# Two layers of attention on one core: modulation weights in one-k-tile pieces, other landing times in the planner, other warm-up counts, and the instruction order that follows

## The chip, the cores and the metric

The kernel runs on one core of a Trainium2 chip. The metric is the device time of one execution in microseconds. The core has a matrix engine (PE, with its weight loads listed as PEld), a vector engine (DVE), a scalar engine (ACT), a general engine (POOL) and a queue engine (SP), which issues nearly all transfers from DRAM here. Each engine works through its own list of instructions in order; semaphores tie the lists together.

## The reference

Input x has 256 rows of 1024 numbers, c is one row of 1024. Two layers follow each other, an NSA layer and a MoBA layer. Each is normalised, modulated by a vector computed from c, mixed, and added to x with a gate:

```python
cond = jax.nn.silu(c)
for i in range(DEPTH):
    shift, scale, gate = jnp.split(cond @ ada_w[i] + ada_b[i], 3, axis=-1)
    h = rms_norm(x, norm_g[i]) * (1 + scale[:, None, :]) + shift[:, None, :]
    y = mixer(h, ...)
    x = x + gate[:, None, :] * y
```

The first mixer projects h by w_in (queries, six key and value blocks, gate logits, an output gate z), compresses keys and values into 15 blocks, selects blocks, attends in three ways, multiplies by silu(z) and projects by w_out. The second has one causal attention over the 256 rows with the same z and w_out. All matrices are float32. The products of h with a weight are made of three products of rounded parts: with hi the rounded number and lo the rest, hi times hi, hi times lo and lo times hi.

## The kernel before, in words

Contraction runs over 1024 = 8 k tiles of 128. A tile `HT` holds h transposed, hi and lo, for all 8 k tiles. Weight pieces are loaded into buffers of 128 x 1024 floats (`early`, 12 of them, in the first stage; `raw`, 5, later), ACT casts a piece to `hi` (four buffers), DVE subtracts to get `lo` (four buffers), and PE multiplies.

**The first stage** (from line 1216 on, `START`) builds h of layer 0 in pieces of two k tiles, because the modulation weights arrive in pieces too. `load_stage("s", k0)` loads eight 256 KB pieces, one for each k tile of c, holding shift and scale for the h tiles k0 and k0+1. For k0 = 0 and 6 `ada_start` turns them into a row with products on PE (tile `ps<-early,condz`), copies it to SBUF (ACT, tile `row`) and transposes it (`ada_columns`); for k0 = 2 and 4 `ada_summed` adds the eight pieces up on DVE (eight operations on `row`, 128 x 512 each) and sums over partitions on PE with a column of ones. Either way DVE then writes the columns `AB`, and ACT (hi) and DVE (through `rot`, lo) write two k tiles of `HT`. `load_stage("k", k0)` loads the NSA weights of two k tiles in four pieces: ci 0 (key and value before compression, goes to `acc`), ci 1 and 2 (the other keys and values) and ci 3 (256 columns of queries, half the size).

**Later modulation** (the gate of layer 0 and shift and scale of layer 1) comes from `ada_rows`, called three times. It adds up eight k tiles of a 1 x 1024 row in one PSUM tile, four products for each k tile, each on 32 columns of the array. A piece is 512 KB.

**Warm-up.** `SPINS` products whose result nobody reads are put on PE twice: on x (`ps<-X,identF`) before the first modulation products, and on the first `row` (`ps<-row,identF`).

**The order.** Nothing is issued as it is written. `Plan` records every operation and `issue` lays them out with a list scheduler: per engine it takes, among the operations that can start, the one with the lowest number in `TURNS` (one number for each operation, some 2400). When an operation can start comes from a cost model inside the kernel: for a load, the time on the wire (`RATE`, with factors for short rows such as 1.06) plus `LANDED`. These figures, `TURNS` and the buffer counts fix the order of each engine when the kernel is built; on the chip nothing is chosen any more. All operations carry line 543 (545 after the change), where the recorded calls are issued, so rows are told apart by their tiles.

Of the kernel before, what the change touches and what calls it, by code (L numbers as in the profile page):

```python
# [18 lines left out]
P = 128  # L19
S = 256  # L20
D = 1024
# [18 lines left out]
WRITTEN = 2500.0  # L40
TURNS = [
# [528 lines left out]
def kernel(  # L570
# [265 lines left out]
    def ada_rows(l, cs):  # L836

        acc = tile_of("ps", 256)
        for kk in range(0, 8, 2):
# [4 lines left out]
            if kk < 6:  # L844
                yield
# [860 lines left out]
```

## Time and profile before

| | us |
|---|---|
| median of 3 runs | 311.52 |
| lowest, highest | 309.72, 1549.1 |
| the profiled execution | 312.38 |
| its span, first to last instruction | 310.7 |
| PE busy in it | 290.5 |
| DVE busy in it | 254.9 |
| ACT busy in it | 195.9 |

The profiled execution took 312.38 us, its span 310.7 us; the 1.7 us between lie around the first and last instruction. Times inside the profile are counted from the first instruction. In the timeline a row merges instructions of the same kind that follow each other: its start, how long the row lasts, engine, operation, output tile and input tiles, shape, count, and in brackets how long the engine sat idle before it and what ended that. A product of float32 operands leaves two records. "x16" of the 32-column products is 8 products.

### The profile page before, as it was taken

How to read it: one execution, taken by the hardware profiler on the slowest of the kernel's cores; microseconds unless marked ns; L12 is line 12 of the kernel's file. 1: busy time of each engine (PE TensorE's matmuls, PEld its weight loads, DVE VectorE, ACT ScalarE, POOL GpSimd, SP SyncE). 2: the span in 40 equal slices, each digit the busy share in tenths (PEclk: the TensorE clock that was granted, in tenths of full speed). 3: DMA queues.
4: the chain of work that ended last, by engine and by line, in shares of the span. 5: the costliest groups of instructions: out<-in, count | busy, mean ns of one | idle time of the engine just before them, and what ended most of it. 6: DMA issues, size and time to landing. Idle time of an engine off the chain costs nothing.

```text
span 310.7 us, 6923 instructions
## 1 busy us (share of the span) xinstructions
PE 290.5 (93%) x2597; PEld 238.7 (77%) x2597; DVE 254.9 (82%) x529; ACT 195.9 (63%) x467; POOL 27.7 (9%) x99
## 2 busy tenths in 40 slices
PE   4679999999999998999998999989998998999995
PEld 4567877787766777788778887767886997997884
DVE  2279984679994798899986978896799999999965
ACT  4364351484457747999658935768593898399530
POOL 7000007890000000000000000010000000000000
PEclk9999989999999999999999999999999999999999
DMA  7999999256979978394999799433789673467603
GB/s 261 293 361 354 346 365 364 82 166 198 354 214 333 324 210 256 126 340 167 361 270 204 176 228 302 184 92 113 208 262 312 203 214 126 138 142 197 138 0 135
DMA packets 49728, 70.83 MB, mean 228 GB/s; under 512 B 4908, under 2 KB 29087, under 8 KB 49696
## 3 DMA queue, kind: packets, MB, share of 16 engines
q1 hardware_dynamic: 49528, 70.34, 72.8%
q8 instruction: 20, 0.33, 0.5%
q14 instruction: 12, 0.10, 0.1%
q10 hardware_dynamic: 168, 0.06, 0.1%
HBM read 67.76 MB, written 2.62 MB: 227 GB/s over the span
## 4 chain that ended last, share of the span: by engine, by line
PE 56%; DVE 19%; DMA 13%; ACT 5%; issue 4%; SPq 1%; ACTq 0%; DVEq 0%
PE ps L543 34%; PE acc L543 22%; DVE lo L543 7%; DVE p L543 5%; DMA raw<-in_ada_w_dram 4%; DMA raw<-in_moba_w_in_dram 3%; DMA early<-in_nsa_w_in_dram 3%; DMA raw<-in_nsa_w_in_dram 2%; ACT hi L543 2%; DMA y<-in_norm_g_dram 2%; SPq L543 1%; DVE tiny L543 1%; DVE row L543 1%; ACT p L543 1%; DVE rs L543 1%
## 5 line engine op out<-in xcount | busy, mean ns | idle before, releaser
L543 ACT CAST hi<-raw 128x1024 fp32r<-128x1024 f32 (+1 forms) x50 | 51.3, 1030 | 19.9 <-PE acc L543 8.5
L543 DVE TENSOR_TENSOR lo<-raw,hi 128x1024 fp32r<-128x1024 f32 (+1 forms) x50 | 58.8, 1183 | 4.4 <-ACT hi L543 4.3
L543 PE MATMUL acc<-HT,hi 128*128 128x256 f32 x256 | 50.8, 289 | 1.8 <-DVE zT L543 1.4
L543 PE MATMUL acc<-hi,HT 128*128 128x512 f32 (+1 forms) x160 | 50.3, 383 | 0.8 <-ACT HT L543 0.8
L543 ACT ACTIVATE p<-ps,tiny 128x128 f32<-128x128 f32 (+1 forms) x96 | 39.9, 447 | 6.7 <-DVE tiny L543 6.6
L543 PEld LDWEIGHTS acc<-HT,hi 128*128 128x128 f32 x256 | 40.5, 189 | 4.3 <-DVE zT L543 1.8
L543 PE MATMUL acc<-HT,lo 128*128 128x256 f32 x128 | 36.2, 289 | 0.0
L543 PE MATMUL ps<-hi,HT 128*128 128x512 f32 (+1 forms) x112 | 35.2, 381 | 0.5 <-ACT HT L543 0.5
L543 PEld LDWEIGHTS acc<-hi,HT 128*128 128x128 f32 x160 | 28.9, 188 | 7.5 <-ACT HT L543 1.0
L543 PE MATMUL acc<-lo,HT 128*128 128x512 f32 (+1 forms) x80 | 30.4, 385 | 1.3 <-DVE lo L543 1.3
L543 PE MATMUL ps<-KTA,qg 128*128 128x256 f32 (+1 forms) x192 | 29.6, 288 | 0.0
L543 DVE TENSOR_REDUCE tiny<-ps 128x2 f32<-128x512 f32 (+2 forms) x40 | 24.4, 627 | 4.3 <-PE ps L543 2.8
L543 PEld LDWEIGHTS ps<-KTA,qg 128*128 128x128 f32 x192 | 25.8, 190 | 1.5 <-issue 1.2
L543 ACT CAST hi<-early 128x1024 fp32r<-128x1024 f32 (+1 forms) x17 | 14.7, 894 | 17.9 <-PE ps L543 8.7
L543 PEld LDWEIGHTS ps<-hi,HT 128*128 128x128 f32 x112 | 21.1, 195 | 5.6 <-ACT HT L543 1.4
L543 PEld LDWEIGHTS acc<-HT,lo 128*128 128x128 f32 x128 | 23.9, 189 | 1.1 <-DVE rs L543 0.4
L543 PE MATMUL ps<-hi,qg 128*128 128x256 f32 (+1 forms) x96 | 23.7, 326 | 1.0 <-ACT hi L543 1.0
L543 ACT ACTIVATE p<-p,tiny 128x256 f32<-128x256 f32 x48 | 22.1, 544 | 1.6 <-DVE tiny L543 1.6
L543 DVE TENSOR_TENSOR lo<-early,hi 128x1024 fp32r<-128x1024 f32 (+1 forms) x17 | 17.2, 1033 | 7.2 <-ACT hi L543 7.2
L543 DVE STREAM_TRANSPOSE p<-p 128x1536 f32<-128x1536 f32 x12 | 21.1, 1768 | 1.9 <-ACT p L543 1.7
L543 ACT ACTIVATION_READ_ACCUMULATOR p<-ps,tiny 128x1 f32 x96 | 22.2, 231 | 0.0
L543 PE MATMUL ps<-lo,HT 128*128 128x512 f32 (+1 forms) x56 | 21.4, 383 | 0.3 <-DVE lo L543 0.3
(199 smaller groups left out, 550.4 us busy)
## 6 DMA issues: line engine op xcount, KB each, us to landing
raw<-in_ada_w_dram SPq DMA_DIRECT2D x32, 512.0 KB
early<-in_ada_w_dram SPq DMA_DIRECT2D x32, 256.0 KB
early<-in_nsa_w_in_dram SPq DMA_DIRECT2D x12, 512.0 KB
raw<-in_moba_w_in_dram SPq DMA_DIRECT2D x12, 512.0 KB
raw<-in_nsa_w_in_dram SPq DMA_DIRECT2D x20, 256.0 KB
raw<-in_nsa_cmp_w_dram SPq DMA_DIRECT2D x8, 512.0 KB
raw<-in_nsa_w_out_dram SPq DMA_DIRECT2D x16, 256.0 KB
raw<-in_moba_w_in_dram SPq DMA_DIRECT2D x16, 256.0 KB
```

The costliest lines, as they stand in the source:

```text
L543: getattr(self.engines[op["engine"]], method)(*[self._real(a) for a in args], **{k: self._real(a) for k, a in kw.items()})
```

## The change

Four things in the code, and a new order that comes out of them:

1. `ada_rows` loads its pieces by a new helper, `ada_blocks`. A piece held two k tiles of one 512-column block, and a pair of k tiles needed two pieces; now a piece holds one k tile of both column blocks. There are 8 pieces of 512 KB in a call as before. The products of one k tile (four) form a group of their own, where those of two k tiles (eight) did.
2. The planner's figures: weights of the first stage are planned to land 1900 ns after the wire (`BEHIND`) in place of 700, and rows of up to 256 floats count 1.1 times their bytes in place of 1.06. These two change no instruction by themselves.
3. Eleven warm-up products on x in place of eight, six on the row in place of eight.
4. A new `TURNS`, for the new list of operations.

```diff
+BEHIND = 1900.0
 TURNS = [
-    53, 54, 47, 55, 56, 57, 2, 9, 7, 8, 58, 52, 14, 71, 3, 5, 4, 6, 0, 1, 11, 28, 59, 43, 29, 30, 41, 2344, 20, 21, 45,
...
-SPINS = 8
+SPINS = (11, 6)
...
+    def ada_blocks(l, kk, cs):
+
+        apart = cs[1] - cs[0]
+        w = load(bass.AP(tensor=ada_w.tensor, offset=ada_w.offset + (l * D + kk * P) * 3 * D + cs[0],
+                         ap=[[3 * D, P], [1, 1024]] if apart == 512 else [[3 * D, P], [apart, 2], [1, 512]]), "raw")
+        return w if apart == 512 else w.rearrange("p s n -> p (s n)")
...
         acc = tile_of("ps", 256)
-        for kk in range(0, 8, 2):
-            w = [ada_piece(l, kk, c0, 512) for c0 in cs]
+        for kk in range(8):
+            w = ada_blocks(l, kk, cs)
             with plan.at(FILL), plan.group():
-                for k in (kk, kk + 1):
-                    ada_step(acc, k, [w[j // 2][:, k % 2, 256 * (j % 2):256 * (j % 2) + 256] for j in range(4)])
-            if kk < 6:
+                ada_step(acc, kk, [w[:, 256 * j:256 * j + 256] for j in range(4)])
+            if kk in (1, 3, 5):
                 yield
```

Where the order moved, at the three places that matter below. A number behind a tile's name tells the buffers and tiles of one kernel apart and says nothing across kernels.

ACT, from the copy of the first transposed x tiles to the first casts of weights. Before, hi_265 is made of the ci 1 weights and hi_292, in two halves, of the ci 0 weights, which the first dense products use:

```order
L543 COPY p_234<-ps_227 128x4x128
L543 CAST hi_265<-early_217 128x1024
L543 COPY row_285<-ps_236 128x128
L543 CAST hi_292<-early_247 128x512 x2
L543 ACTIVATE HT<-p_234,AB_130 128x256 x2
L543 COPY p_319<-ps_169 128x4x128
```

ACT after; early_235 holds the ci 0 weights, early_267 the ci 1 weights:

```order
L545 COPY p_269<-ps_169 128x4x128
L545 COPY row_280<-ps_211 128x128
L545 ACTIVATE HT<-p_250,AB_130 128x256 x2
L545 CAST hi_305<-early_235 128x512 x2
L545 COPY p_269<-ps_240 128x4x128
L545 CAST hi_323<-early_267 128x1024
```

The copy of the modulation row and the two writes of HT now stand ahead of every cast of a weight, and ci 0 is cast (and loaded) ahead of ci 1.

DVE, the same stretch, up to the lo part of the last weights of the first two k tiles. Before, lo_277 is of ci 1, lo_304 of ci 0, lo_340 of ci 3, lo_385 of ci 2; the operations on row are the sum of `ada_summed` for k0 = 2:

```order
L543 TENSOR_TENSOR lo_277<-early_217,hi_265 128x1024
L543 TENSOR_TENSOR AB_130<-ps_204,RT 128x2 x2
...
L543 TENSOR_TENSOR lo_304<-early_247,hi_292 128x512 x2
...
L543 TENSOR_TENSOR lo_340<-early_267,hi_325 128x512
L543 SCALAR_TENSOR_TENSOR row_285<-early_232,condz,row_285 128x512
L543 SCALAR_TENSOR_TENSOR row_285<-early_279,condz,row_285 128x512 x2
L543 SCALAR_TENSOR_TENSOR row_285<-early_288,condz,row_285 128x512 x2
L543 SCALAR_TENSOR_TENSOR row_285<-early_308,condz,row_285 128x512
L543 TENSOR_TENSOR lo_385<-early_331,hi_372 128x1024
```

DVE after; lo_312 is of ci 0, lo_334 of ci 1, lo_369 of ci 3, lo_382 of ci 2:

```order
L545 TENSOR_TENSOR AB_130<-ps_195,RT 128x2 x2
...
L545 TENSOR_TENSOR lo_312<-early_235,hi_305 128x512 x2
L545 TENSOR_SCALAR row_280<-early_284,condz 128x512
L545 SCALAR_TENSOR_TENSOR row_280<-early_284,condz,row_280 128x512
L545 TENSOR_TENSOR lo_334<-early_267,hi_323 128x1024
L545 SCALAR_TENSOR_TENSOR row_280<-early_252,condz,row_280 128x512 x2
L545 SCALAR_TENSOR_TENSOR row_280<-early_303,condz,row_280 128x512 x2
L545 SCALAR_TENSOR_TENSOR row_280<-early_330,condz,row_280 128x512
L545 TENSOR_TENSOR lo_369<-early_338,hi_365 128x512
L545 SCALAR_TENSOR_TENSOR row_280<-early_330,condz,row_280 128x512
L545 TENSOR_TENSOR lo_382<-early_344,hi_374 128x1024
```

AB no longer stands behind a weight's lo part, and the small piece ci 3 gets its lo part after seven operations of the sum where it was after one.

PE, where the gate of layer 0 is computed beside the first z block. Before, in eights (two k tiles); raw_625 and raw_662 hold the third pair of k tiles:

```order
L543 MATMUL ps_169<-raw_705,condz 32x256 x2
L543 MATMUL ps_169<-raw_683,condz 32x256 x2
L543 MATMUL ps_169<-raw_705,condz 32x256 x2
L543 MATMUL ps_169<-raw_683,condz 32x256 x2
...
L543 MATMUL ps_227<-TCS,selC 64x32 x2
...
L543 MATMUL ps_169<-raw_625,condz 32x256 x2
L543 MATMUL ps_169<-raw_662,condz 32x256 x2
L543 MATMUL ps_169<-raw_625,condz 32x256 x2
L543 MATMUL ps_169<-raw_662,condz 32x256 x2
```

PE after, in fours (one k tile); raw_699, raw_598 and raw_709 hold k tiles 2, 3 and 4, raw_662 k tile 5:

```order
L545 MATMUL ps_211<-raw_699,condz 32x256 x4
L545 MATMUL ps_211<-raw_598,condz 32x256 x4
L545 MATMUL ps_211<-raw_709,condz 32x256 x4
L545 MATMUL acc_317<-HT,lo_382 128x256
...
L545 MATMUL ps_211<-TCS,selC 64x32 x2
L545 MATMUL ps_211<-raw_662,condz 32x256 x4
```

Three k tiles now stand in one run where two did; over all three calls of `ada_rows` the k tiles stand in 12 runs, before in 11.

## Rows read from the trace of the kernel before

**Rows 1.** The head of the profile's page: the span, and each engine's busy time with its share and its instructions.

```profile
span 310.7 us, 6923 instructions
PE 290.5 (93%) x2597; PEld 238.7 (77%) x2597; DVE 254.9 (82%) x529; ACT 195.9 (63%) x467; POOL 27.7 (9%) x99
```

**Rows 2.** Busy time by stretches of 10 us: the stretch, its length, busy us and instructions of PE, PEld, DVE, ACT, POOL, then the granted PE clock, the DMA engines' busy share and GB/s.

```profile
0.00:10.00 10.00, 4.35 (x19) 3.97 (x20) 4.07 (x22) 4.42 (x8) 5.96 (x33) 1.00 0.82 269
10.00:20.00 10.00, 7.86 (x97) 6.47 (x96) 2.80 (x8) 4.28 (x8) 0.00 (x0) 1.00 0.99 323
20.00:30.00 10.00, 9.32 (x45) 6.92 (x45) 9.68 (x17) 5.97 (x9) 0.00 (x0) 1.00 1.05 360
30.00:40.00 10.00, 10.00 (x47) 8.18 (x47) 9.64 (x18) 3.66 (x5) 0.00 (x0) 1.00 1.05 346
300.00:310.00 10.00, 6.95 (x42) 5.97 (x40) 5.75 (x10) 0.00 (x0) 0.00 (x0) 1.00 0.29 105
```

**Rows 3.** The timeline of PE in the first 40 us.

```profile
4.25 3.78 PE L543 MATMUL ps<-X,identF 128*128 128x128 f32 x16 [0.91 <-DMA X<-in_x_dram]
...
9.83 1.94 PE L543 MATMUL ps<-identF,n_in 128*128 128x128 f32 x8 [1.64 <-DVE n_in L543]
...
14.46 1.08 PE L543 MATMUL ps<-early,condz 128*32 128x128 f32 x32 [0.56 <-DMA early<-in_ada_w_dram]
...
20.39 0.49 PE L543 MATMUL acc<-hi,HT 128*128 128x512 f32 x1 [0.78 <-ACT HT L543]
...
28.75 0.50 PE L543 MATMUL ps<-lo,HT 128*128 128x512 f32 x1 [0.26 <-DVE lo L543]
...
29.50 1.02 PE L543 MATMUL ps<-ones,row 128*128 128x1 f32 x8
```

**Rows 4.** The timeline of ACT in the first 40 us.

```profile
15.80 1.04 ACT L543 CAST hi<-early 128x1024 fp32r<-128x1024 f32 x1 [3.41 <-DMA early<-in_nsa_w_in_dram]
16.75 0.26 ACT L543 COPY row<-ps 128x128 f32<-128x128 f32 x1
18.70 1.14 ACT L543 CAST hi<-early 128x512 fp32r<-128x512 f32 x2 [1.69 <-DMA early<-in_nsa_w_in_dram]
19.75 1.09 ACT L543 ACTIVATE HT<-p,AB 128x256 fp32r<-128x256 f32 x2
```

**Rows 5.** The timeline of DVE in the first 40 us.

```profile
16.88 1.23 DVE L543 TENSOR_TENSOR lo<-early,hi 128x1024 fp32r<-128x1024 f32 x1 [6.63 <-ACT hi L543]
18.02 0.22 DVE L543 TENSOR_TENSOR AB<-ps,RT 128x2 f32<-128x2 f32 x2
...
19.35 1.29 DVE L543 TENSOR_TENSOR lo<-early,hi 128x512 fp32r<-128x512 f32 x2 [0.54 <-ACT hi L543]
...
21.88 0.48 DVE L543 TENSOR_SCALAR row<-early,condz 128x512 f32<-128x512 f32 x1
22.27 0.68 DVE L543 TENSOR_TENSOR lo<-early,hi 128x512 fp32r<-128x512 f32 x1
22.88 4.68 DVE L543 SCALAR_TENSOR_TENSOR row<-early,condz,row 128x512 f32<-128x512 f32 x6
27.47 1.22 DVE L543 TENSOR_TENSOR lo<-early,hi 128x1024 fp32r<-128x1024 f32 x1
28.61 0.74 DVE L543 SCALAR_TENSOR_TENSOR row<-early,condz,row 128x512 f32<-128x512 f32 x1
...
31.01 0.22 DVE L543 TENSOR_TENSOR AB<-ps,RT 128x2 f32<-128x2 f32 x2
```

**Rows 6.** The chain of waits that ended last, in order of time (start, length, what): one link of the first stage.

```profile
10.51 8.17 DMA early<-in_nsa_w_in_dram
```

**Rows 7.** The timeline of PE from 38 us on, and then busy time by stretches of 1 us with columns as in rows 2.

```profile
41.57 0.95 PE L543 MATMUL ps<-ones,row 128*128 128x1 f32 x8
...
43.15 0.99 PE L543 MATMUL ps<-y,ones 1*128 1x432 f32 x2
...
43.00:44.00 1.00, 1.00 (x4) 0.30 (x3) 1.00 (x3) 1.00 (x3) 0.00 (x0) 1.00 1.11 358
44.00:45.00 1.00, 1.00 (x4) 0.79 (x4) 0.86 (x3) 1.00 (x3) 0.00 (x0) 0.72 1.09 347
45.00:46.00 1.00, 1.00 (x4) 0.79 (x3) 0.86 (x3) 0.93 (x1) 0.17 (x1) 0.50 1.08 359
46.00:47.00 1.00, 1.00 (x4) 0.72 (x3) 0.00 (x0) 0.00 (x0) 1.00 (x4) 0.50 1.07 385
47.00:48.00 1.00, 1.00 (x4) 0.81 (x3) 0.00 (x0) 0.00 (x0) 0.73 (x4) 0.58 1.04 382
```

**Rows 8.** A link of the chain of waits, and the timeline of PE, around the gate of layer 0.

```profile
113.03 6.37 DMA raw<-in_ada_w_dram
...
119.45 1.07 PE L543 MATMUL ps<-raw,condz 128*32 128x256 f32 x16 [1.04 <-DMA raw<-in_ada_w_dram]
```

**Rows 9.** The timeline of PE at two runs of modulation products, of 16 and of 32 records, each with the row after it.

```profile
109.37 1.07 PE L543 MATMUL ps<-raw,condz 128*32 128x256 f32 x16
110.37 0.51 PE L543 MATMUL acc<-HT,hi 128*128 128x256 f32 x2
...
143.79 1.93 PE L543 MATMUL ps<-raw,condz 128*32 128x256 f32 x32
145.65 0.38 PE L543 MATMUL acc<-HT,hi 128*128 128x256 f32 x1
```

**Rows 10.** The timelines of DVE and PE in layer 1, at three waits of PE.

```profile
204.25 1.22 DVE L543 TENSOR_TENSOR lo<-raw,hi 128x1024 fp32r<-128x1024 f32 x1
...
209.67 1.39 PE L543 MATMUL ps<-identF,n_in 128*128 128x128 f32 x8 [0.18 <-DVE n_in L543]
...
236.01 1.29 DVE L543 SCALAR_TENSOR_TENSOR gate<-raw,condz,gate 128x1024 f32<-128x1024 f32 x1 [0.55 <-DMA raw<-in_ada_w_dram]
...
238.57 0.50 PE L543 MATMUL acc<-lo,HT 128*128 128x512 f32 x1 [1.04 <-DVE lo L543]
...
259.38 0.38 PE L543 MATMUL acc<-HT,hi 128*128 128x256 f32 x1 [0.69 <-DVE zT L543]
```

More of the change, by code (lines that the diff above doesn't have):

```diff
@@ L296, in record @@
             op["bytes"] = self.bytes
-            op["landed"] = WRITTEN if str(args[0].space).endswith("DRAM") else SMALL if engine == "A" and aps[1].shape[0] > 8 else LANDED
+            op["landed"] = WRITTEN if str(args[0].space).endswith("DRAM") else SMALL if engine == "A" and aps[1].shape[0] > 8 else BEHIND if aps[0].tensor.name.startswith("early") and aps[1].tensor.name.startswith("in_nsa_w_in") else LANDED
         if engine == "T":
@@ L320, in _cost @@
             if self.bytes > 1e5:
-                self.bytes *= SHORT_ROWS if row <= 128 else 1.06 if row <= 256 else 1.0
+                self.bytes *= SHORT_ROWS if row <= 128 else 1.1 if row <= 256 else 1.0
                 self.bytes *= HALF_WIDTH if aps[0].shape[0] <= P // 2 else 1.0
@@ L722 @@
     with plan.at(FILL):
-        for _ in range(SPINS):
+        for _ in range(SPINS[0]):
             T.matmul(spin[:, 0:P], identF, X[:, 1, 0:P], start=True, stop=True)
@@ L909, in ada_start @@
             with plan.at(FILL):
-                for _ in range(SPINS):
+                for _ in range(SPINS[1]):
                     T.matmul(spin[:, P:2 * P], identF, g, start=True, stop=True)
```

234 rows, old and new, of the table TURNS are left out of this document.

## The prediction

> **What bounds the kernel now.** I read the head of the page first. PE is busy 290.5 of 310.7 us and DVE 254.9 [rows 1], so PE sets the time, and all that a change can win without taking work from PE is PE's idle time, 310.7 - 290.5 = 20.2 us. Next come the stretches of 10 us. The first two hold 5.65 + 2.14 = 7.8 us of that idle and the last full one 3.05 [rows 2]; between 20 and 300 us some 9 us are spread thinly. DVE is full from 20 on too (9.68 of 10) and the DMA engines carry 323 to 360 GB/s from 10 to 40 us [rows 2]. A faster front therefore meets two other full resources. The timeline of PE says what ends the waits of the front: x, n_in, modulation weights, the row, HT [rows 3].
>
> The first dense product starts at 20.39 after 0.78 of waiting for ACT's HT [rows 3]. ACT wrote HT at 19.75, directly after the cast of ci 0 (18.70, held 1.69 by a transfer), and it copied the row at 16.75 directly after the cast of ci 1 (15.80) [rows 4]. That ci 0 transfer was issued at 10.51 and took 8.17 [rows 6]. DVE made AB at 18.02, directly behind the lo of ci 1 [rows 5].
>
> The clock is the third thing to see. It stands at 1.00 of 2.4 GHz nearly everywhere, but falls to 0.50, which is 1.2 GHz, around 45 us, while PE is listed as busy 1.00 of each us [rows 7]. The rows there lose 0.28 + 0.50 + 0.50 + 0.42 = 1.70 us. What PE did before the fall is the sum with the ones column (0.95 for 1-column products) and a product with one output row (0.99) [rows 7].
>
> **The front, part by part.** *Removed waits.* The last group of modulation products starts at 14.46 and takes 0.54 (1.08 for two groups) [rows 3], so the row can be copied at about 15.0 and not 16.75: ACT no longer has a cast ahead of it. With the 0.26 of the copy [rows 4], transposes as before (AB follows 0.95 after the copy's start less what the lo took; I take 0.8), AB stands at 16.0 and HT at 16.6, and ci 0, now the first weights to be issued, is cast at about 17.7 if it lands like the first of before (15.80 [rows 4]). The first dense product comes at about 18.3, a lead of 2.1 us.
>
> *What takes the lead back.* DVE has the same operations in another order. From AB to the first SCALAR_TENSOR_TENSOR it needed 22.88 - 18.02 = 4.86 [rows 5]; without the 0.61 of the ci 3 lo (22.27 to 22.88) that is 4.25, so the first of these starts at 16.0 + 4.25 = 20.25. From there after's row of work: one at (27.47 - 22.88) / 6 = 0.765 [rows 5], to 21.0; lo of ci 1, 28.61 - 27.47 = 1.14 [rows 5], to 22.15; five more of the sum, 3.83, to 26.0; lo of ci 3, 0.61, to 26.6; one more of the sum to 27.4; lo of ci 2, 1.14, to 28.5. PE meanwhile has the 24 products of ci 0 and ci 1. At some 0.235 each (two in the 0.49 + 0.39 that overlap, 20.39 to 20.73 with the first's latency; the mean of 20.39 to 28.75 with its half-width ones is near it) 14 of them end at 21.6, it waits 0.5 for the lo of ci 1, ten more end at 24.6, and then the lo of ci 3 is missing until 26.6: 2.0 us of waiting that before did not have. Twelve half-width products later the lo of ci 2 is awaited once more (about 0.4, before 0.26 [rows 3]). The sum with the ones stands behind four ci 2 products, at about 29.5; before it started at 29.50 [rows 3] with the same 36 products of ci 0, 1 and 3 done. AB for the next two k tiles, 31.01 before [rows 5], cannot move. So I book **-0.3** for the front, between -1.1 (half the lead passes, if DVE's operations start a little earlier than I sum) and +1.7 (the wait at 24.6 costs clock, below).
>
> *Warm-up.* A product on x leaves two records, 16 take 3.78 [rows 3], so three more add 6 x 0.236 = 1.4 us, and they lie in the 1.64 that PE waits for n_in before 9.83 [rows 3]: **0**; were n_in ready earlier, up to +1.4 minus the slack, at most 0.2 as things stand. Two fewer on the row come out of 0.78 of idle before 20.39: **0**. The clock was 1.00 at 10 to 20 us [rows 2] and loses nothing by them.
>
> **The modulation pieces.** Each is 512 KB as before and there are as many, so DMA time and issues are unchanged: **0** on SP. What moves is when a k tile is complete. Before, the third pair of k tiles waited 1.04 at 119.45 for a transfer of 6.37 [rows 8]. After, tiles 2, 3 and 4 stand in one run ahead of that place and tile 5 behind two small works. A k tile needs one piece and not two, so the last product of a run hangs on fewer transfers; I book **-0.8** of the 1.04. Bounds: -1.04 (all of it) and +5.3 (the run of three reaches its last piece a whole transfer early: 6.37 - 1.04).
>
> A run of 16 records takes 110.37 - 109.37 = 1.00 to the next row's start, one of 32 takes 145.65 - 143.79 = 1.86 [rows 9], so 16 records cost 0.86 and a run 0.14 of its own. One run more (12 for 11) with a change of shape before and after it: **+0.25**, between 0.14 and 0.5.
>
> **Layer 1.** At 204.25 a lo of 1.22 stands ahead of the work that ends PE's small wait at 209.67; the gate's operation (236.01, 1.29 long, itself 0.55 late) stands right ahead of the lo that PE awaits at 238.57 for 1.04; and 0.69 is lost at 259.38 for zT [rows 10]. In after the order around the latter two is the same; at the first, one lo less stands in DVE's way and five fewer products cover it. **0**, between -0.7 and +1.0.
>
> Sum: -0.3 - 0.8 + 0.25 = -0.85. The profiled execution took 312.38 with a span of 310.7; it lies 0.86 above the median of 311.52. So 311.5 for a run like the profiled one, and **310.7** for the median.
>
> **A rule against the trace.** The rows show the clock falling at 44.3 us out of stretches in which PE is busy 1.00 [rows 7]. In after the same two pieces of small products stand at the same place, with three or four full-width products between them where five half-width ones stood, so I let the 1.70 stay. The Trainium skill, TensorE: Matmul & The Clock Gate, "Part 1: The HAM clock gate", says that the lower level is what the engine has by default and that activity lifts it, and that it returns after idling. By that rule alone the fall at 44.3 would not have come at all and the profiled run would have been 1.7 shorter; the trace does not agree. The same rule would have the clock fall at a real wait such as the one I expect at 24.6, which is the second rival.
>
> **The rivals.** *First, the clock stays up or the lead passes through (0.25).* The fall at 44 us hangs on what lies between two sums; other neighbours may avoid it (-1.7), or half the lead of the front survives (-1.1). For it: the lowest of the runs shown, 309.72, lies 1.8 below the median, about the size of one fall. Against it: the two pieces are still close together. Time: 310.7 - 1.7 = 309.0, with both 307.9.
>
> *Second, slower: PE's new wait for the lo of ci 3 (0.18).* DVE puts seven operations of the sum ahead of a 0.61 us lo. If PE idles there for 2 us after the 0.5 at 21.6, the clock falls for some us as it does at 44, for 1.7, with what DVE is late besides (0 to 1). It decides from the point where PE's idle between 20 and 30 passes the 0.68 of before [rows 2] by more than the 2.1 of the lead. Time: 312.4 to 313.4. For it: DVE's sum is longer than PE's cover by 2.0. Against it: before, PE lost 2.14 between 10 and 20 us [rows 2] in pieces and kept 1.00.
>
> *Third, the new order closes waits all over (0.09).* All 2,400 numbers are new. Half of the 9 us of thin idle gone, and the forecast's own: 310.7 - 4.5 = 306.2; with the clock 304.5. Against it: PE is the engine that is full, and its waits have different causes.
>
> *Fourth, the run of three k tiles waits for a whole transfer (0.04).* +5.3 and the 0.8 not won: 316.8, with a fall of the clock 318.5. Against it: `raw` has five buffers as before.
>
> *That the change does nothing* is inside the forecast: its own range is 310.0 to 312.0.
>
> **How the numbers follow.** Forecast 0.44 at 310.7. The range for 8 in 10 takes in the forecast, the first and second rival and half of the third: 305.5 to 314.0. Two per cent, about what a measurement here tells from no change, is 6.2 us: below 305.3 or above 317.8. Faster by that much: the third rival with the clock and some of what lies between, 0.10. Slower: the fourth with its fall, and a second fall with several late waits, 0.05. Within: 0.85.
>
> **What would show it.** First dense product at about 18.3, row copy before any cast: the removed waits. A wait of PE for a lo at about 24.6, and the ones sum at 29.5 again: the lead is taken back by DVE; if the sum stands near 28 my order of DVE's ends is wrong. Clock at 0.50 somewhere between 40 and 50: the fall stays. No wait over 0.3 for raw around 119: the gate term. The forecast is wrong if the clock falls in two places, or in none, or if PE between 50 and 300 us is idle by over 2 us more or less than before.

## The result and the profile after

The changed kernel's median is 310.17 us (20 runs, 306.42 to 312.81), the kernel before's beside it 311.82 us. The ratio is **0.993, 95% interval 0.9904 to 0.9956**: some 2.2 us faster, well inside 2%. The ratio leaves out disturbed, slower executions; the medians do not, and differ by 1.65. The prediction had 310.7, range 305.5 to 314.0, and a gain of 0.85. So time and range held, but the gain is two and a half times the size forecast (twice by the medians). The profiled execution took 309.16 us. Its page begins:

```profile
span 307.4 us, 6941 instructions
PE 288.7 (94%) x2599; PEld 237.7 (77%) x2599; DVE 255.2 (83%) x529; ACT 195.9 (64%) x467; POOL 29.3 (10%) x99
```

Against [rows 1] the engines have the same work, with two records of PE more for one warm-up product. PE's idle time falls from 20.2 to 307.4 - 288.7 = 18.7 us. That is 1.5 of the 3.3 us by which the span is shorter. For the other 1.8 PE is listed as busy for less time, which the waits below do not account for. The timeline of PE, the front first:

```profile
17.93 0.73 PE L545 MATMUL acc<-hi,HT 128*128 128x512 f32 x2 [0.72 <-ACT hi L545]
19.05 0.50 PE L545 MATMUL acc<-lo,HT 128*128 128x512 f32 x1 [0.39 <-DVE lo L545]
...
25.78 0.39 PE L545 MATMUL ps<-lo,HT 128*128 128x256 f32 x1 [1.22 <-DVE lo L545]
...
29.08 0.95 PE L545 MATMUL ps<-ones,row 128*128 128x1 f32 x8
...
40.30 1.05 PE L545 MATMUL ps<-ones,row 128*128 128x1 f32 x8
...
111.25 0.37 PE L545 MATMUL ps<-TCS,selC 128*64 128x32 f32 x4
...
118.73 1.07 PE L545 MATMUL ps<-raw,condz 128*32 128x256 f32 x16 [1.39 <-DMA raw<-in_ada_w_dram]
...
142.35 1.50 PE L545 MATMUL ps<-raw,condz 128*32 128x256 f32 x24 [0.45 <-DMA raw<-in_ada_w_dram]
...
235.75 0.50 PE L545 MATMUL acc<-lo,HT 128*128 128x512 f32 x1 [1.34 <-DVE lo L545]
...
256.88 0.39 PE L545 MATMUL acc<-HT,hi 128*128 128x256 f32 x1 [0.90 <-DVE zT L545]
```

DVE and ACT in the front of this kernel, from their timelines:

```profile
15.24 0.23 DVE L545 TENSOR_TENSOR AB<-ps,RT 128x2 f32<-128x2 f32 x2 [4.84 <-PE ps L545]
...
25.04 0.68 DVE L545 TENSOR_TENSOR lo<-early,hi 128x512 fp32r<-128x512 f32 x1
...
30.07 0.23 DVE L545 TENSOR_TENSOR AB<-ps,RT 128x2 f32<-128x2 f32 x2 [0.39 <-PE ps L545]
```

```profile
14.55 0.27 ACT L545 COPY row<-ps 128x128 f32<-128x128 f32 x1 [2.35 <-PE ps L545]
```

The first dense product comes 2.46 us earlier (20.39 in [rows 3]), the two sums with ones 0.42 and 1.27 earlier (29.50, 41.57 in [rows 3, 7]). At the products with selC next to nothing is left: before did them at 111.20, as the next fence of PE rows shows, though with one k tile of the gate less done ahead of them. From there a new lead grows: 2.82 us at the wait for lo (238.57 in [rows 10]) and 2.50 at the wait for zT (259.38). Before, three waits stood between:

```profile
111.20 0.37 PE L543 MATMUL ps<-TCS,selC 128*64 128x32 f32 x4
...
162.21 0.39 PE L543 MATMUL acc<-HT,hi 128*128 128x256 f32 x1 [0.42 <-ACT hi L543]
...
170.62 0.63 PE L543 MATMUL ps<-hi,qg 128*128 128x256 f32 x2 [0.97 <-ACT hi L543]
...
192.41 0.39 PE L543 MATMUL ps<-lo,qg 128*128 128x256 f32 x1 [0.53 <-DVE lo L543]
```

None of these three is in the changed kernel's trace. Summed over rows of 10 us, PE's idle time between 160 and 200 us falls from 2.08 to 0.22, while between 100 and 160 it grows from 1.57 to 2.05. The busy time by stretches of 10 us (columns as in [rows 2]) says what changed just ahead of them, before and then after:

```profile
140.00:150.00 10.00, 10.00 (x107) 8.07 (x105) 9.41 (x20) 8.52 (x36) 0.00 (x0) 1.00 0.61 222
```

```profile
140.00:150.00 10.00, 9.55 (x126) 6.92 (x132) 8.99 (x18) 8.80 (x35) 0.00 (x0) 1.00 0.87 291
```

The DMA engines are at 0.87 where they were at 0.61. In this stretch the pieces for shift and scale of layer 1 go through `raw`, and the weights of the output projections are queued behind them on SP. I had priced the pieces at the gate of layer 0 alone.

### The profile page after: what moved, and what is told of

Same layout as the page of the kernel before. It is cut to its first block, busy times and chain, and to the rows that moved or that the text cites. A ratio compares the mean times of both kernels' runs of the same rounds, so it can differ in the third digit from the quotient of the medians.

```text
span 307.4 us, 6941 instructions
## 1 busy us (share of the span) xinstructions
PE 288.7 (94%) x2599; PEld 237.7 (77%) x2599; DVE 255.2 (83%) x529; ACT 195.9 (64%) x467; POOL 29.3 (10%) x99
## 4 chain that ended last, share of the span: by engine, by line
PE 60%; DVE 19%; DMA 13%; issue 3%; ACT 3%; SPq 1%; ACTq 0%; DVEq 0%
PE ps L545 34%; PE acc L545 26%; DMA raw<-in_ada_w_dram 6%; DVE lo L545 5%; DMA early<-in_ada_w_dram 4%; DVE p L545 3%; DVE rs L545 2%; DMA y<-in_nsa_cmp_pe_dram 2%; DVE tiny L545 2%; ACT hi L545 1%; DVE y L545 1%; DMA raw<-in_nsa_cmp_w_dram 1%; DVE row L545 1%; DVE KTA L545 1%; DVE X L545 1%
## 5 line engine op out<-in xcount | busy, mean ns | idle before, releaser
L545 PE MATMUL acc<-hi,HT 128*128 128x512 f32 (+1 forms) x160 | 51.3, 386 | 1.4 <-ACT hi L545 1.2
L545 PE MATMUL acc<-HT,hi 128*128 128x256 f32 x256 | 49.3, 287 | 1.1 <-DVE zT L545 0.9
L545 PE MATMUL ps<-hi,HT 128*128 128x512 f32 (+1 forms) x112 | 34.5, 381 | 0.0
L545 PE MATMUL ps<-hi,qg 128*128 128x256 f32 (+1 forms) x96 | 22.9, 321 | 0.1
L545 PE MATMUL acc<-hi,qg 128*128 128x512 f32 x64 | 21.7, 401 | 0.0
L545 ACT ACTIVATE p<-p,tiny 128x256 f32<-128x256 f32 x48 | 21.2, 522 | 0.6 <-DVE tiny L545 0.6
L545 ACT ACTIVATION_READ_ACCUMULATOR p<-ps,tiny 128x1 f32 x96 | 21.0, 218 | 0.0
```

The source lines that it names most:

```text
L545: getattr(self.engines[op["engine"]], method)(*[self._real(a) for a in args], **{k: self._real(a) for k, a in kw.items()})
```

## The experiments

Two theories stood at the start: (1) the gain comes from the new order behind 140 us, (2) the front is the gain. Theory 3 of the expectations is, in e1, that the front's lead is absorbed, and in e3 that the pieces by themselves are the gain. To keep an order while one part is changed, the scheduler's choice was replaced by a fixed list of operations, taken in turn as each becomes ready; the text below says whose list each kernel follows. No run repeats the changed kernel with its own list fixed; nearest to that is e8, with one step moved, and it gives 0.9927. Each ratio is to executions of before beside that run.

| run | front | pieces gate / shift, scale | ratio to before | 95% interval |
|---|---|---|---|---|
| the change | new | new / new | 0.993 | 0.9904 to 0.9956 |
| e1 | new | old / old, old order | 1.0021 | 0.9983 to 1.0058 |
| e2 | old | new / new, new order | 0.9929 | 0.9894 to 0.9964 |
| e3 | old | new / new, old order | 0.9957 | 0.9925 to 0.9988 |
| e4 | old | old / old, new order | 1.0028 | 0.9994 to 1.0062 |
| e5 | new | old / old, new order | 1.005 | 1.0019 to 1.0082 |
| e6 | new | new / old, new order | 1.0018 | 0.9984 to 1.0052 |
| e7 | new | old / new, new order | 0.9955 | 0.9918 to 0.9991 |
| e8 | new | as the change, one DVE step moved | 0.9927 | 0.9897 to 0.9957 |
| e9 | new | old, a group for each piece | 1.0075 | 1.0035 to 1.0115 |
| e10 | new | new, groups of eight | 0.995 | 0.9911 to 0.9989 |
| e11 | new | as e8, and two los of the front | 0.9922 | 0.9886 to 0.9959 |
| e12 | new | new, eights in shift and scale | 0.997 | 0.9926 to 1.0013 |

**e1, the front alone.** The kernel before, its list up to the second ones sum replaced by the new one, and

```diff
-    SPINS = 8
+    SPINS = (11, 6)
```

> The kernel before with the warm-up counts 11 and 6 and, up to the sum for the third pair of k tiles (about 41 us), the order of the changed kernel; everything behind that, and the modulation pieces, as before. If the front's lead passes to the end (theory 1): 0.5 to 1.0 us faster than before, ratio 0.997 to 0.998, first dense product near 17.9 and PE still 0.5 to 1.0 ahead of before at 130 us. Theory 2 (the whole gain is the front): ratio 0.993. Theory 3 (the lead is absorbed, as the prediction had it): 0.999 to 1.001, with the lead gone by the second ones sum or by 60 us.

Ratio 1.0021: no gain. The timeline of PE in this kernel, and then one row of before:

```profile
17.38 0.73 PE L531 MATMUL acc<-hi,HT 128*128 128x512 f32 x2 [0.73 <-ACT hi L531]
...
81.80 0.66 PE L531 MATMUL ps<-identF,y 128*128 128x128 f32 x4 [0.64 <-ACT y L531]
...
159.22 0.63 PE L531 MATMUL ps<-KTA,qg 128*128 128x256 f32 x4 [1.06 <-issue]
...
237.00 0.50 PE L531 MATMUL acc<-lo,HT 128*128 128x512 f32 x1 [1.64 <-DVE lo L531]
```

```profile
84.56 0.66 PE L543 MATMUL ps<-identF,y 128*128 128x128 f32 x4 [0.64 <-ACT y L543]
```

The execution of before lost 1.70 us to the clock [rows 7] and this one did not, so 1.70 comes off each lead. The first dense product is 3.01 us earlier than in [rows 3] (there the clock has not fallen yet), at the wait for y 84.56 - 81.80 - 1.70 = 1.06 are left, and at 237.00 (238.57 in [rows 10]) nothing. The lead went into the longer waits from 159 us on (1.64 where [rows 10] has 1.04). It is absorbed as the prediction said, but it outlives 60 us.

**e2, everything but the front.** The changed kernel with the front in the order of before and the old counts:

```diff
-    SPINS = (11, 6)
+    SPINS = (8, 8)
```

> The changed kernel with warm-up counts 8 and 8 and the front (up to about 41 us) in the order of before; pieces and the rest of the order as changed. Theory 1 (the gain comes from the new order behind 140 us, where PE no longer waits for casts): ratio to before 0.994 to 0.996. Theory 2 (front alone): 0.999 to 1.001. The wait of 0.97 for ACT's hi that before shows at 170.62 is gone in this kernel by theory 1.

Ratio 0.9929, the whole gain. Theory 2 falls; the front is worth nothing that these intervals (some 0.35% or 1.1 us to either side) can show, with e1 from both sides. The wait for ACT near 170 us is gone, as theory 1 had it. The share of the DMA engines, though, is hardly above the 0.61 of before:

```profile
140.00:150.00 10.00, 9.07 (x123) 6.60 (x127) 8.50 (x17) 8.35 (x34) 0.00 (x0) 1.00 0.67 228
```

As the mean of the three rows from 130 to 160 us it is 0.80 in before, 0.83 in e2 and 0.88 in the changed kernel. So a single stretch of one execution is a hint and not a measure of the gain.

**e3, the pieces alone**, in the order of before; its edit is the change's own in `ada_rows`, nothing else.

> The modulation pieces of one k tile in the order of before: each new load stands where an old one stood, the two new groups of four stand where one group of eight stood; warm-up 8 and 8. Theory 1 and 2: no difference, ratio 0.999 to 1.002 (a k tile waits for one piece and not two, but the group pair stands together). Theory 3 (pieces by themselves are the gain): 0.993 to 0.996, with the wait of 1.04 at 119.45 smaller by half or more.

Ratio 0.9957. Its interval ends below 1, so the pieces help even without the new order, which theories 1 and 2 did not expect. The wait at the gate is gone: no wait over 0.3 us for raw is left between 100 and 160 us of its trace, and none for ACT near 170. In the order of before the pieces are thus worth some 1.3 us, 0.4 to 2.3 by the interval.

**e4, the new order with old pieces.** The kernel before, its list behind 41 us replaced.

> The kernel before with its old pieces and warm-up 8 and 8, front as before, and behind 41 us the order of the changed kernel, a group of eight products standing where the second of two groups of four stands. If the new order is worth its gain without the new pieces: ratio 0.994 to 0.996, as the run with the new pieces. If the one-k-tile pieces are what makes that order good: 0.998 or above, and waits of PE for a raw modulation piece between 100 and 160 us of over 1 us.

Ratio 1.0028. Theory 1 falls: the order by itself brings no gain. The wait for raw that it was expected to show is there, and the one for ACT near 170 too:

```profile
142.09 1.92 PE L531 MATMUL ps<-raw,condz 128*32 128x256 f32 x28 [1.91 <-DMA raw<-in_ada_w_dram]
...
170.43 0.62 PE L531 MATMUL ps<-hi,qg 128*128 128x256 f32 x2 [0.80 <-ACT hi L531]
```

**e5 to e7, which pieces.** The changed kernel with its own list; e5 has the old loop of `ada_rows` everywhere, e6 for l = 1 (shift, scale), e7 for l = 0 (gate). In e7:

```diff
-        for kk in range(8):
-            w = ada_blocks(l, kk, cs)
...
+        if l == 1:
+            for kk in range(8):
+                w = ada_blocks(l, kk, cs)
...
+        else:
+            for kk in range(0, 8, 2):
+                w = [ada_piece(l, kk, c0, 512) for c0 in cs]
```

> The changed kernel, its front, warm-up and order kept, with the old modulation pieces (two k tiles of one block) in place of the new. If the new pieces carry the gain (theory P): ratio to before 0.999 to 1.004. If the rest of the change carries it: 0.992 to 0.995.

> The same, but the gate of layer 0 uses the new pieces (here their rows in DRAM are 4 KB, where the old ones have 2 KB) and shift and scale of layer 1 the old. If what matters is the longer rows, or the wait at the gate: 0.993 to 0.997. If what matters is that a k tile hangs on one transfer and its buffer comes free by itself in the densest stretch, 130 to 160 us: 0.998 to 1.002, with the waits of PE for raw at 142 and for ACT's hi near 170 still there.

> The mirror: shift and scale of layer 1 with new pieces (their rows stay 2 KB), the gate of layer 0 with old. If the buffers and waits between 130 and 160 us carry the gain: 0.993 to 0.997 and the wait near 170 gone. If the longer rows or the gate carry it: 0.998 to 1.002.

Old pieces in this order cost 1.005; new ones at the gate alone make it 1.0018, a difference inside the intervals; new ones for shift and scale alone 0.9955, whose interval is clear of e5's. So of the 1.005 - 0.993 = 1.2% (3.7 us) that the pieces are worth in this order, 0.95% (3.0 us) is reached by shift and scale alone. Their rows in DRAM are 2 KB with either kind of piece, so longer rows are not what carries it. PE and the DMA engines at this place, in e5:

```profile
140.86 0.63 PE L532 MATMUL ps<-raw,condz 128*32 128x256 f32 x4
143.40 1.92 PE L532 MATMUL ps<-raw,condz 128*32 128x256 f32 x28 [1.92 <-DMA raw<-in_ada_w_dram]
```

```profile
140.00:150.00 10.00, 7.98 (x78) 4.93 (x77) 7.50 (x13) 7.77 (x33) 0.00 (x0) 1.00 0.47 143
```

and in e7:

```profile
139.25 0.64 PE L533 MATMUL ps<-raw,condz 128*32 128x256 f32 x8
141.00 1.50 PE L533 MATMUL ps<-raw,condz 128*32 128x256 f32 x24 [0.21 <-DMA raw<-in_ada_w_dram]
```

```profile
140.00:150.00 10.00, 9.79 (x197) 7.73 (x203) 9.15 (x19) 8.89 (x36) 0.00 (x0) 1.00 0.86 293
```

SP's issues of these pieces, in e5 and then in e7 (start, how long the run of issues lasts):

```profile
128.64 26.82 SPq L532 DMA_DIRECT2D raw<-in_ada_w_dram  x14
```

```profile
126.92 24.58 SPq L533 DMA_DIRECT2D raw<-in_ada_w_dram  x14
```

With old pieces PE does 4 records, two of a k tile's four products, and then stands for the second piece, with the first one's buffer still held; SP, which issues in order, is held up longer (its 14 issues take 26.82 us; between 126 and 156 us it waits 18.6 us for PE's products, 16.3 in e7), and the DMA engines drop to 0.47. With new pieces 8 records, a whole k tile, go through on one transfer, the next run waits 0.21, and the issues are done in 24.58.

These rows compare two kinds of piece in the new order. They are not what parts the change from before: the same 14 issues took 24.15 us before and take 24.42 in the changed kernel, and PE was busy 10.00 of 10 between 140 and 150 us before. The wait of 1.92 came with the new order.

```profile
130.18 24.15 SPq L543 DMA_DIRECT2D raw<-in_ada_w_dram  x14
...
128.43 24.42 SPq L545 DMA_DIRECT2D raw<-in_ada_w_dram  x14
```

**e8, a wait of layer 1.** One move in DVE's list of the changed kernel:

```diff
+TENSOR_TENSOR lo<-raw,hi 128x1024
 SCALAR_TENSOR_TENSOR gate<-raw,condz,gate 128x1024
-TENSOR_TENSOR lo<-raw,hi 128x1024
```

> The changed kernel with one DVE operation moved: the first product of layer 1's gate with raw (233.19, which waited 0.97 for its transfer) stands behind the lo that PE awaits for 1.34 at 235.75, not ahead of it. If that wait is the order's and nothing takes its place: 0.8 to 1.3 us faster than the changed kernel, ratio to before 0.989 to 0.991. If the next late thing (a buffer that the moved operation frees, zT at 257) takes it back: 0.992 to 0.994 as the changed kernel, and the wait at 257 grows by what 235 loses.

Ratio 0.9927, the second case. The wait of 1.34 at 235.75 is gone, the one for zT did not grow (0.86), but a new one stands between, in PE's timeline:

```profile
241.76 0.54 PE L533 MATMUL ps<-identR,lo 128*128 128x128 f32 x4 [0.75 <-DVE lo L533]
...
255.64 0.39 PE L533 MATMUL acc<-HT,hi 128*128 128x256 f32 x1 [0.86 <-DVE zT L533]
```

So 0.75 of the 1.34 is taken back within 6 us by DVE's next lo. The 0.6 that would be left is less than these intervals resolve.

**e9 and e10, group or shape.** e9 keeps the old pieces and makes a group of each:

```diff
+            for c in range(2):
+                w = ada_piece(l, kk, cs[c], 512)
+                with plan.at(FILL), plan.group():
+                    for k in (kk, kk + 1):
+                        for j in (2 * c, 2 * c + 1):
```

e10 keeps the new pieces and puts two k tiles in a group again:

```diff
-            w = ada_blocks(l, kk, cs)
+            w = [ada_blocks(l, kk + c, cs) for c in range(2)]
```

> The changed kernel with the old pieces (two k tiles of one block, 2 KB rows), but a group of four products per piece where the old kernel put eight products of two pieces in a group; each group stands where a group of the changed kernel stands. If what counts is that a group hangs on one transfer and its buffer comes free with it (theory B): ratio to before 0.992 to 0.996, DMA share near 0.85 between 140 and 150 us, no wait of PE for raw over 1 us near 142. If the shape of the new piece itself counts: 1.002 to 1.005, as the old pieces in this order gave.

> The changed kernel with the new pieces, but the eight products of two k tiles in one group again, standing where the second of two groups stands now. Theory B: the gain is gone, ratio to before 1.002 to 1.006, PE waits 1.5 to 2 us for raw near 142 and the DMA share between 140 and 150 us is near 0.5. If the shape of the piece counts: 0.992 to 0.996.

Both came out the other way than theory B had it: 1.0075 and 0.995. e9 is no clean test, as its rows show (and its wait for raw is 1.18, where theory B had none over 1):

```profile
141.23 1.06 PE L533 MATMUL ps<-raw,condz 128*32 128x256 f32 x8
144.37 1.92 PE L533 MATMUL ps<-raw,condz 128*32 128x256 f32 x24 [1.18 <-DMA raw<-in_ada_w_dram]
```

Its 8 records use two of the four 32-column parts of the array and last 1.06, where 8 records on all four last 0.64 (above, e7). That cost was left out of its expectation. e10's trace has the waits that theory B named, though its time has not lost the gain:

```profile
140.32 0.64 PE L532 MATMUL ps<-raw,condz 128*32 128x256 f32 x8
...
142.54 1.50 PE L532 MATMUL ps<-raw,condz 128*32 128x256 f32 x24 [1.58 <-DMA raw<-in_ada_w_dram]
...
170.00 0.62 PE L532 MATMUL ps<-hi,qg 128*128 128x256 f32 x2 [1.35 <-ACT hi L532]
```

Its DMA share between 140 and 150 us is 0.74, where theory B had some 0.5. A group is only an order, not a joint wait: in e10 the first k tile's four products (140.32) still run on one piece, and the rest waits 1.58 us behind them. What separates e10 (0.995) from e5 (1.005) is the shape of the piece, at the same grouping and nearly the same list, and the intervals do not touch.

**e11, two places of DVE's order.** As e8, and in the front the lo of ci 3 ahead of two operations of the sum, the lo of ci 2 ahead of one.

> The changed kernel with two places of DVE's order changed: in layer 1 the lo ahead of the gate's product as in the run before, and in the front the lo of ci 3 ahead of two, the lo of ci 2 ahead of one of the operations of the sum. If the front's waits are DVE's and a lead there reaches the end: PE's wait of 1.22 at 25.78 falls below 0.4, and the whole is 0.989 to 0.991 of before. If a lead of the front is absorbed behind 100 us, as the run with the front alone said: the wait falls all the same, the lead is there at 42 us, and the ratio is that of the run with one lo moved, 0.992 to 0.994.

```profile
27.32 0.49 PE L533 MATMUL ps<-lo,HT 128*128 128x512 f32 x1 [0.78 <-DVE lo L533]
...
40.05 1.05 PE L533 MATMUL ps<-ones,row 128*128 128x1 f32 x8
```

The wait of 1.22 is gone and 0.78 stands 1.5 us later, at the next lo; the second sum is 0.25 earlier than in the changed kernel. Ratio 0.9922: the same as e8 and as the change. It is not shown to beat them.

**e12, eights for shift and scale only.** The gate's groups stay as changed; two groups of four move on PE beside their partners.

> The changed kernel, all pieces new, the gate's groups as changed; only shift and scale of layer 1 have their eight products of two k tiles in one group again. In the order this moves two groups of four: the first half of a pair stands beside its second half, some ten rows later or earlier on PE. Theory B (in the stretch from 130 to 170 us a group that hangs on one transfer gives the buffer back early): ratio to before 1.000 to 1.004, PE waits over 1 us for raw near 142 and the wait for ACT's hi near 170 is back. If the piece's shape carries that stretch, or the grouping is worth little: 0.992 to 0.996.

Ratio 0.997, between the two cases; its interval reaches into both. Of the two waits that theory B named the one near 170 came back, the one near 142 did not:

```profile
168.35 0.62 PE L533 MATMUL ps<-hi,qg 128*128 128x256 f32 x2 [0.95 <-ACT hi L533]
```

So the grouping in shift and scale is worth between nothing and some 0.8% (1.0013 - 0.993), by these runs.

## Why the prediction was right, and where not

**The front, booked -0.3: right, and its working nearly so.** Row copy at 14.55, ahead of all casts, first dense product at 17.93 (18.3 forecast), PE's new wait for the lo of ci 3 from 24.56 on (24.6) and 1.22 long (2.0), ones sum at 29.08 (29.5). DVE's sum was read from the right rows, but AB, which "cannot move", moved from 31.01 to 30.07, as DVE ran 1.0 ahead of my sums (its lo of ci 3 at 25.04 and not at 26.0), most of it because the first AB stood at 15.24 and not at 16.0. It came 0.69 after the start of the row copy, where I had put 0.26 and 0.8; the 0.95 that I took the 0.8 from is not in the rows (before, AB follows the copy's start by 18.02 - 16.75 = 1.27). The lead of 0.9 to 1.3 at 41 us is then lost further back. e1 and e2 put the front's worth at nothing that they can resolve, from both sides.

**The warm-up counts, 0: nothing speaks against it.** They were tried only with the front's order, in e1 and e2, and these show no effect.

**The gate, booked -0.8: misread, and the term failed in its place.** The run that waits at 119.45 is not the third pair of k tiles. Three runs of the gate stand ahead of it, that at 109.37 [rows 9] and these two, so it is the fourth and last pair:

```profile
101.28 1.07 PE L543 MATMUL ps<-raw,condz 128*32 128x256 f32 x16
...
111.94 1.07 PE L543 MATMUL ps<-raw,condz 128*32 128x256 f32 x16
```

The tiles 2 to 5 that I reasoned about are done before it; tiles 6 and 7 stand in one run of 16 records before and after. The wait there grew from 1.04 to 1.39. It varies, one execution each: in other kernels with this order and new pieces at the gate it is 0.34 (e11) to 1.10 (e12), and nowhere the 0.3 or less that I had named as the sign. In the order of before the new pieces do remove it (e3, 0.23 left). The fourth rival, that a run of three waits for a whole transfer, did not come about.

**The extra run, booked +0.25: too much, by these two traces.** The 192 records of these products are busy 12.8 us in 11 runs before and 12.9 us in 12 runs now. The change of shape costs nothing there: a run of 24 records lasts 1.50 and one of 8 0.64, so 16 and 16 records (1.07 each [rows 9]) come as 24 and 8 for the same 2.14.

**The mis-sized step is the pieces.** I wrote that what moves is when a k tile is complete, and then priced it only where before shows a wait for raw, at 119.45 [rows 8], and added the terms as if each stood alone. In the new order the runs show the larger part, 0.95% or 3.0 us of 3.7, in shift and scale, where before shows no wait for raw at all: its waits are those for ACT and DVE at 162 to 192, downstream. Part of these 3.7 us makes good what the new order costs with old pieces. In the order of before the pieces are worth some 1.3 us (e3), and the 0.8 lies inside that run's interval. What I had not read is the DMA share, 0.61 between 140 and 150 us. SP has loads queued there: between 126 and 156 us of before it waits 10.8 us for PE's products and 8.1 for DVE's lo, which read from these buffers. That buffers freed late are what makes the waits downstream is argued from this and not shown: in the changed kernel SP waits as long for both together (16.3 and 3.1), and e2 has the gain at a share of 0.67.

**The new order, 0: right within the noise by itself (e4), wrong as a sum of parts.** With old pieces it is 0.28 to 0.5% slower than before (e4, e5; only e5's interval is clear of 1), with new pieces it stands at 0.993 against 0.9957 in the old order, which the intervals don't tell apart. Pieces and order cannot be priced apart. The heads of the pages hint at how they meet, one execution each. PE's idle time (span less busy) is 22.4 and 22.2 us in e4 and e5, 18.4 in e3 and 17.4 in e2. Its busy time, in executions without a fall of the clock, is 289.2 and 290.5 us in the order of before (e1, e3) and 287.4 to 288.7 in the new one (e4, e5, e7). So the new order may shorten PE's busy time and lengthen its waits, and the new pieces take the waits back; no run was made to test this. That the changed kernel's busy time is 1.8 us shorter speaks against my first premise, that idle time is all that can be won at the same work. The third rival, half of the thin waits closed, did not come: PE's idle time between 50 and 300 us went from 8.04 to 6.69, inside the 2 us that I had allowed.

**The clock, booked as staying: right in this execution and not for the reason given.** The changed kernel's profile has the fall again, at 43 to 47 us, and no second one while PE works:

```profile
44.00:45.00 1.00, 1.00 (x4) 0.81 (x3) 0.90 (x3) 0.50 (x1) 0.00 (x0) 0.50 1.09 346
```

But e1 to e7 have none at this place, with the same pieces of small products there, and of the changed kernel's 20 executions eight have a mean granted clock of 0.998 or more, twelve one of 0.992 to 0.994. The first rival thus named an accident of the single execution, and the second, a fall at the wait for the lo of ci 3, came in no trace: the clock stays at 1.00 through the wait of 1.22, and through 1.69 of the same wait in e9:

```profile
26.18 0.38 PE L533 MATMUL ps<-lo,HT 128*128 128x256 f32 x1 [1.69 <-DVE lo L533]
```

Nor is it the clock that makes the change faster. In executions with a mean granted clock of 0.997 or more the median is 312.19 us for before (11 of those beside e1 to e4), 309.04 for e2 (5) and 310.15 for e3 (4); 311.52 for e5 (7) and 309.44 for e7 (5).

What stays open: what in the shape of the piece makes e10 faster than e5. Between 100 and 160 us PE is idle 4.84 us in e5 and 2.58 in e10. The wait near 142 is not much of it (1.92 and 1.58); the one at the gate is more, in e5 and then in e10:

```profile
118.44 1.17 PE L532 MATMUL ps<-raw,condz 128*32 128x256 f32 x16 [1.81 <-DMA raw<-in_ada_w_dram]
...
116.41 1.07 PE L532 MATMUL ps<-raw,condz 128*32 128x256 f32 x16 [0.74 <-DMA raw<-in_ada_w_dram]
```

Against that, e10 waits 1.35 near 170, and e5 has no such wait. The gate's rows, 4 KB in place of 2 KB, could be a part of it; e6 says that it is a small one in this order. It was not tried with 2 KB rows in new pieces.

## What to carry to other kernels

Where a ring of buffers feeds an engine, look at the DMA share of the stretch and not only at the waits for the ring: here 0.61 with loads queued stood ahead of waits for something else, 12 to 50 us later. It says where to try, not what will be won. Cut a piece so that what is computed from it needs no second piece, and so that its products still use all parts of the array (e9). Do not add up a new order and a new piece as if each had its own price. A lead won at the start is worth what is left of it after the next stretch that waits on another resource; follow it to the end of the kernel before booking it.

## What the runs showed of the hardware

The granted clock fell to half for some 3.5 us in six of the 14 profiled executions, at 40 to 50 us in three (before, the change, e8), at 120 to 130 us in e2 and e10, at 140 to 150 us in e6, and in eight nowhere between 20 and 300 us. Kernels with the same list around the place had it or not (e5 to e7 share the changed kernel's front), so it goes with the execution and not with the order alone. In e10:

```profile
120.00:130.00 10.00, 10.00 (x81) 7.76 (x80) 7.06 (x9) 9.21 (x27) 0.00 (x0) 0.83 0.57 177
```

PE is listed as busy 10.00 of 10 there: in these rows no idleness of PE stands ahead of the fall. In e6 a wait of 1.85 for raw ends at 142.05, just ahead of the fall, but in e5 one of 1.92 at the same place brought none. Besides these, the clock falls behind PE's last product, where it costs PE nothing; in the changed kernel:

```profile
303.00:304.00 1.00, 0.75 (x7) 0.54 (x5) 0.94 (x3) 0.00 (x0) 0.00 (x0) 1.00 0.18 68
...
306.00:307.00 1.00, 0.00 (x0) 0.00 (x0) 0.00 (x0) 0.00 (x0) 0.00 (x0) 0.50 0.04 8
```

The Trainium skill, TensorE: Matmul & The Clock Gate, "Part 1: The HAM clock gate", lets the lower level return after idling; the fall at the end agrees with it, those of before [rows 7] and e10 do not agree with it as the only cause.

The second: four products on two of the four 32-column parts last 1.06 us, on all four 0.64 (e9, e7), for the same number of columns.
